# The opening rounds of a hybrid DeltaNet and sparse-attention decoder step: another order for blocks, splits, modulation tiles, block weights and constants

## The chip, the cores and the metric

The kernel runs on one core of a Trainium2 chip. Its engines work in parallel, each through its own queue of instructions in order: TensorE (PE; its weight loads are shown as PEld), VectorE (DVE), ScalarE (ACT), GpSimd (POOL) and SyncE (SP), which issues most of the transfers. The metric is the device time of one execution in microseconds; 2323.8 is the median of three runs of the kernel before.

## The reference, cut to what matters

One layer: a modulated, normalised input `h` goes through one wide projection `w_in`, feeds two branches (gated DeltaNet, and attention over keys that an indexer selects), and their merge goes through an output projection.

```
mod = einsum('bc,cd->bd', silu(c), w_ada) + b_ada        # 9 conditionings, 2048 x 6144
shift, scale, gate = split(mod, 3)
h = rms_norm(x, pre_norm_g) * (1 + scale) + shift        # 256 prompt + 64 sample tokens
(a_qkv, a_z, a_b, a_a, b_q, b_k, b_v, b_z, i_q, i_k, i_w, g_a, g_b) = split_columns(h @ w_in)
y_a = gdn_branch(a_qkv, a_z, a_b, a_a, ...)
y_b = attend(b_q, b_k, b_v, i_q, i_w, i_k) * silu(b_z)
merged = sigmoid(g_a) * (y_a @ w_pa) + sigmoid(g_b) * (y_b @ w_pb)
out = x + gate * rms_norm(merged @ w_out, post_norm_g)
```

All is float32. `h` is needed by every product with `w_in`, and it needs `shift` and `scale`, which are two thirds of the product with `w_ada`: 32 MB of weights for 9 rows.

## The kernel before

The 320 tokens (256 prompt, 64 sample) lie along the free axis. An operand of 128 features is kept as two parts, `xh` (rounded to a format that TensorE takes in one pass) and `xl` (the remainder); weights are split in the same way into `whi`/`wlo`, by ScalarE (a copy that rounds) and VectorE (the difference). A product of one 128 x 128 block is three matmuls: hi by xh, hi by xl, lo by xh.

`build` plans a stream of chunks of `w_in`, `w_pa`, `w_pb` and `w_out`. A chunk is 256 columns in two half tiles `raw` of 1 MB each; it gives four units of 24 matmuls (`stream`), each unit with its own `whi`/`wlo`. `split_ahead` keeps two units split ahead, `load_ahead` asks for `raw` tiles when one of three is free. Attention, recurrence and gates are generators beside the stream; `side_round` runs them in the middle and at the end of a unit, when a model of the engines' clocks (`Clock`) says that their inputs are ready. The order of instructions on every engine's queue is the order in which the program emits them.

`startup` comes ahead of the stream. It has eight rounds. Round q takes two column blocks of `w_ada` (256 columns of shift, 256 of scale), in four tiles of 1 MB (`rawx`, `raw`), through a ring of six buffers, three of its own and the three `raw` tiles. The product with the conditionings `cT` uses four 32-column groups of the array at once; "columns" below means these products, 64 instructions per round, 16 per tile. Their sums in `pm` are copied to `msb`, four matmuls with `sel` add the groups, VectorE makes `mod` and `gs`, and `operand` transposes two blocks of `x` and makes two 128-feature blocks of `xh` and `xl` (helper `hT`).

`first_blocks(q)` uses the two feature blocks of round q for the first 720 columns of `w_in` (step sizes, indexer weights and key, attention's k and v): a tile `awr` of 128 x 2 x 720, filled by four transfers per round, split into `awh` and `awl`, and 36 matmuls into six accumulators `ps`. In round q the order is: all columns of round q, the copy to `msb`, `first_blocks(q-1)` with its split at its head, selection, operands. Two PSUM banks (`ps_main`) serve columns, selection and transposes in turn.

The requests for tiles come from `load`, which is called after the columns and in `first_blocks`; it asks for block weights as early as two modulation tiles ahead of the count. After the rounds `attention` opens its buffers, loads the page table, makes row numbers (`idx`), a selection matrix `esel`, masks and constants on POOL and VectorE, and starts the side work; only then are the six accumulators copied out and the stream begins.

Nearly every instruction of the trace has line 56, that of a helper which records all operations, so groups are told apart by tile names.

Of the kernel before, what the change touches and what calls it, by code (L numbers as in the profile page):

```python
# [7 lines left out]
F32 = mybir.dt.float32  # L8
F32R = mybir.dt.float32r
BF = mybir.dt.bfloat16  # L10
I32 = mybir.dt.int32
AF = mybir.ActivationFunctionType
OP = mybir.AluOpType
AX = mybir.AxisListType
# [3 lines left out]
NP = 256  # L18
NB, TS = 8, 8
NS = NB * TS  # L20
NT = NP + NS
KB = D // 128
PAGES = 8
# [167 lines left out]
class Kernel:  # L191
# [254 lines left out]
    def startup(self):  # L446
        nc, i = self.nc, self.i
# [17 lines left out]
        def load():  # L465
            while True:
                if st["w"] < min(8, (st["a"] + 2) // 4) and awr.free:
                    load_w()
                if st["a"] == len(seq) or not ring.free:
                    break  # L470
                q, h = seq[st["a"]]
                t = ring.get()
                nc.sync.dma_start(t, wa[1024 * h:1024 * (h + 1), 256 * q:256 * (q + 1)].rearrange(
                    "(k p) c -> p k c", p=128))
                raws[q, h] = t
                st["a"] += 1

        def load_w():
            q = st["w"]
            t = awr.get()  # L480
            for d0, c0, n in ((0, C_BA, 64), (64, C_IW, 16), (80, C_IK, 128), (208, C_BK, 512)):
                nc.sync.dma_start(t[:, :, d0:d0 + n], w[256 * q:256 * (q + 1), c0:c0 + n].rearrange(
                    "(k p) c -> p k c", p=128))
            aws[q] = t
            st["w"] += 1
# [29 lines left out]
        self.sel = self.l0.tile([128, 9], F32, name="sel")  # L515
        nc.vector.tensor_reduce(self.sel, self4, axis=AX.X, op=OP.add)

        junk = self.xh.rearrange("p k t -> p (k t)")[:, 0:D]
# [17 lines left out]
        accs = [self.ps_side.get() for _ in range(6)]  # L536
        blocks = [(0, 80, self.aux_done), (80, 128, self.ik_done)]
        blocks += [(208 + 128 * n, 128, lambda p, n=n: self.bk_done(p, n)) for n in range(2)]
        blocks += [(464 + 128 * n, 128, lambda p, n=n: self.bv_done(p, n)) for n in range(2)]

        def first_blocks(q):
            r = aws.pop(q)
            hi, lo = awh[q % 2], awl[q % 2]
            self.act(hi, r)
            self.tt(lo, r, hi, OP.subtract)
            awr.put(r)
            load()
            for e in range(2):
                kb = 2 * q + e
                for (c0, n, _), acc in zip(blocks, accs):  # L550
                    a = acc[:n, :NT]
                    wh, wl = hi[:, e, c0:c0 + n], lo[:, e, c0:c0 + n]
                    nc.tensor.matmul(a, wh, self.xh[:, kb, :], start=(kb == 0), stop=False)
                    nc.tensor.matmul(a, wh, self.xl[:, kb, :], start=False, stop=False)
                    nc.tensor.matmul(a, wl, self.xh[:, kb, :], start=False, stop=(kb == KB - 1))

        for q in range(8):
            p = self.ps_main.get()
            for e, qq in enumerate((q, 8 + q)):
                for k in range(KB):  # L560
                    j = k % 4
                    self.mm(p[32 * j:32 * j + 32, 256 * e:256 * e + 256], self.cT[:, k, :],
                            raws[qq, k // 8][:, k % 8, :], start=(k < 4), stop=(k >= 12), skip=True)
                for h in range(2):
                    t = raws.pop((qq, h))
                    if q < 6 or t in own:
                        ring.put(t)
                    else:
                        self.raw.put(t)
            load()  # L570
            if q == 7:
                self.load_ahead()
            m = msb
            self.act(m, p)
            self.ps_main.put(p)
            if q == 0:
                p = self.ps_main.get()
                self.tr(p[:, 0:81], rows)
                nc.vector.tensor_copy(self.feat, p[:, 0:81])
                self.ps_main.put(p)  # L580
            if q > 0:
                first_blocks(q - 1)
            p = self.ps_main.get()
            for e in range(4):
                self.mm(p[:, 9 * e:9 * e + 9], m[:, 128 * e:128 * e + 128], self.sel)
            bc = lambda a, n: a.rearrange("p (e o) -> p e o", o=1).to_broadcast([128, n, 9])
            for e, qq in enumerate((q, 8 + q)):
# [5 lines left out]
                     OP.add, OP.mult)  # L593
            for k in (k0, k0 + 1):
                self.operand(k, x, gs, mod, hT[k % 2])
        first_blocks(7)
# [104 lines left out]
    def attn_small(self):  # L701
# [8 lines left out]
        self.att = set()  # L710

    def attention(self):
        nc, a, i = self.nc, self.ap, self.i
        self.qiS = a.tile([128, NB, 128], F32, name="qiS")
# [7 lines left out]
        self.wip = a.tile([128, 2, 16], F32, name="wip")  # L722
        self.esel = a.tile([64, NB, 16, TS], BF, name="esel")
        self.q_r = Ring([a.tile([128, NP], F32, name=f"q{j}") for j in range(6)])
# [4 lines left out]
        self.st = Ring([a.tile([128, 8], F32, name=f"st{j}") for j in range(6)])  # L729

        self.idx = a.tile([128, NB], I32, name="idx")
        pt = a.tile([128, NB], I32, name="pt")
        for s in range(PAGES):
            nc.gpsimd.dma_start(pt[16 * s:16 * s + 16, :],
                                i["page_table"][:, s:s + 1].rearrange("b o -> o b").to_broadcast([16, NB]))
        io = a.tile([128, NB], I32, name="io")
        nc.gpsimd.iota(io, pattern=[[0, NB]], base=0, channel_multiplier=1)
        pgi = a.tile([128, PAGES - 1], I32, name="pgi")
        nc.gpsimd.iota(pgi, pattern=[[-16, PAGES - 1]], base=-16, channel_multiplier=1)
        pgf = a.tile([128, PAGES - 1], F32, name="pgf")  # L740
        nc.vector.tensor_scalar(pgf, pgi, 0.0, None, op0=OP.is_ge)
        page = a.tile([128, 1], F32, name="page")
        nc.vector.tensor_reduce(page, pgf, axis=AX.X, op=OP.add)
        ptf = a.tile([128, NB], F32, name="ptf")
        nc.vector.tensor_scalar(ptf, pt, page, 16.0, op0=OP.subtract, op1=OP.mult)
        self.stt(self.idx, ptf, 1.0, io, OP.mult, OP.add)
        nc.vector.memset(self.esel, 1.0)
        nc.gpsimd.affine_select(self.esel, self.esel, pattern=[[-8, NB], [0, 16], [-1, TS]], compare_op=OP.is_equal,
                                fill=0.0, base=0, channel_multiplier=1)
        self.wi_consts()  # L750
        self.aux_masks()
        self.aux_setup()
# [25 lines left out]

    def wi_consts(self):
        nc, a = self.nc, self.ap  # L780

        self.hsp = a.tile([128, 16, 8], F32, name="hsp")
        e = self.hsp[64:80]
        nc.vector.memset(self.hsp[64:96], 1.0)
        nc.gpsimd.affine_select(e, e, pattern=[[8, 16], [0, 8]], compare_op=OP.is_equal, fill=0.0, base=0,
                                channel_multiplier=-8)
        dti = a.tile([128, 8, 16], I32, name="dti")
        nc.gpsimd.iota(dti, pattern=[[-1, 8], [-8, 16]], base=0, channel_multiplier=1)
        dt = self.s_r.get()
        dtf = dt[:, 0:128].rearrange("p (t h) -> p t h", t=8)  # L790
        nc.vector.tensor_scalar(dtf, dti, 0.0, None, op0=OP.is_equal)
        self.tmask = a.tile([128, 8], F32, name="tmask")
        nc.vector.tensor_reduce(self.tmask, dtf, axis=AX.X, op=OP.add)
        self.s_r.put(dt)

    def aux_masks(self):
        nc, f, a = self.nc, self.fix, self.ap
        g, v, m = nc.gpsimd, nc.vector, self.mask
# [30 lines left out]
    def aux_gen(self):  # L829
# [10 lines left out]
        p = self.psum()  # L840
        self.mm(p[:, 0:64], self.hsp[64:80].rearrange("p h t -> p (h t)"), ax[64:80, NP:NT])
        self.ts(self.wsel, p[:, 0:64].rearrange("p (b t) -> p b t", t=TS), 0.25, None, OP.mult)
        self.tt(self.wsel, self.wsel,
                self.tmask.rearrange("p (o t) -> p o t", o=1).to_broadcast([128, NB, TS]), OP.mult)
        self.ps_side.put(p)
        self.ts(self.wip, xt[:, 0:2, 64:80], 0.25, None, OP.mult)
        self.flags.add("wi")
# [4 lines left out]
        nc.sync.dma_start(al[:, 32:64], i["dt_bias"].to_broadcast([128, 32]))  # L852
        self.act(self.beta, xt[:, :, 0:32], AF.Tanh, scale=0.5)
        self.act(al[:, 0:32], al[:, 0:32], AF.Exp)
# [4 lines left out]
        g = a.tile([128, 3, 32], F32, name="g")  # L859
        self.tt(t1, xt[:, :, 32:64], rep(al[:, 32:64]), OP.add)  # L860
        self.stt(t2, t1, -1.0, t1, OP.mult, OP.min)
# [1273 lines left out]
```

## Time and profile before

| | |
|---|---|
| three runs | 2316.94, 2323.8, 2326.34 us |
| the profiled execution | 2320.8 us, of which the span of the trace is 2319.1 us |
| TensorE busy | 2216.6 us (96% of the span) |
| VectorE, ScalarE, POOL busy | 1368.6, 1013.4, 469.4 us |
| transfers | 432.96 MB, mean 187 GB/s |

Rows of the trace are read like this: windows give busy time of each engine in a stretch with the number of instructions in brackets; a chain row is a start, a duration, and the engine and tile whose work the end of the kernel waited for; a timeline row has a start, a duration, engine, operation, out<-in, and in square brackets the idle time ahead of it and what ended it.

### The profile page before, as it was taken

Reading aid. Unit: us, or ns where it says so; the run is one execution under the profiler, and the core shown is the slowest. Engines: PE = TensorE matmul, PEld = TensorE weight load, DVE = VectorE, ACT = ScalarE, POOL = GpSimd, SP = SyncE. Lnnn points to the kernel's source line nnn. Section 1 sums busy time; section 2 is a strip of 40 time slices with the busy share of each in tenths; the row PEclk is TensorE's granted clock in tenths of the full one; section 3 lists DMA queues with packets and bytes.
Section 4 is the critical chain, followed back from the end, with each engine's and each line's share of the span. In section 5 each row is a group of like instructions: output and inputs, shape, how many; then the busy total and the mean of one; then the engine's idle time right before and its main releaser. Section 6 shows DMA issues by size and latency. Waiting matters only on the chain.

```text
span 2319.1 us, 41332 instructions
## 1 busy us (share of the span) xinstructions
PE 2216.6 (96%) x16448; PEld 2081.1 (90%) x16448; DVE 1368.6 (59%) x2666; ACT 1013.4 (44%) x2191; POOL 469.4 (20%) x624
## 2 busy tenths in 40 slices
PE   5779999999999999999999999999999999999997
PEld 2658997999988999898989898989899999999997
DVE  2323345788844467685868586858665554545433
ACT  2123346443333354554556464546553543333342
POOL 0010000000000007072627162727171000000000
PEclk9878999999999999999999999999999999999999
DMA  9958743434455556475756565656574866644443
GB/s 324 323 162 257 236 162 104 165 110 134 149 202 197 195 177 210 131 237 146 225 169 205 165 208 169 205 168 206 165 231 142 273 210 198 196 153 156 159 142 103
DMA packets 475137, 432.96 MB, mean 187 GB/s; under 512 B 65912, under 2 KB 463880, under 8 KB 472576
## 3 DMA queue, kind: packets, MB, share of 16 engines
q1 hardware_dynamic: 470560, 406.61, 56.3%
q0 software_dynamic: 3840, 21.02, 2.5%
q8 instruction: 129, 2.11, 0.4%
q10 hardware_dynamic: 544, 2.70, 0.3%
q14 instruction: 64, 0.52, 0.1%
HBM read 382.10 MB, written 47.89 MB: 185 GB/s over the span
## 4 chain that ended last, share of the span: by engine, by line
PE 80%; DVE 10%; ACT 4%; POOL 2%; DMA 2%; issue 2%; DVEq 0%; SPq 0%; POOLq 0%; ACTq 0%
PE pm L56 65%; PE ps L56 15%; DVE S L56 2%; DVE wlo L56 2%; DVE ps L56 1%; POOL X L56 1%; ACT whi L56 1%; POOL tmpx L56 1%; DMA raw<-in_w_ada_dram 1%; DMA rawx<-in_w_ada_dram 1%; ACT ot L56 1%; DVE st L56 1%; DVE w L56 1%; DVE awl L56 1%; ACT ps L56 1%
## 5 line engine op out<-in xcount | busy, mean ns | idle before, releaser
L56 PE MATMUL pm<-xh,whi 128*128 128x320 f32 x3328 | 1065.6, 320 | 3.9 <-ACT whi L56 3.9
L56 PE MATMUL pm<-xh,wlo 128*128 128x320 f32 x3328 | 1033.4, 311 | 12.2 <-DVE wlo L56 12.1
L56 PE MATMUL pm<-xl,whi 128*128 128x320 f32 x3328 | 1031.2, 310 | 0.0
L56 DVE TENSOR_TENSOR wlo<-raw,whi 128x1024 fp32r<-128x1024 f32 x480 | 601.9, 1258 | 372.7 <-ACT whi L56 370.9
L56 PEld LDWEIGHTS pm<-xh,whi 128*128 128x128 f32 x3328 | 628.7, 189 | 35.4 <-issue 25.6
L56 PEld LDWEIGHTS pm<-xh,wlo 128*128 128x128 f32 x3328 | 627.9, 189 | 15.2 <-DVE wlo L56 15.0
L56 PEld LDWEIGHTS pm<-xl,whi 128*128 128x128 f32 x3328 | 628.8, 189 | 1.0
L56 ACT ACTIVATE whi<-raw 128x1024 fp32r<-128x1024 f32 x480 | 504.2, 1056 | 261.8 <-PE pm L56 227.5
L56 POOL TENSOR_TENSOR X<-X,tmpx 48x31 f32<-48x31 f32 (+15 forms) x248 | 182.8, 737 | 19.4
L56 POOL TENSOR_TENSOR tmpx<-blk,X 48x31 f32<-48x31 f32 (+15 forms) x248 | 170.7, 688 | 44.3 <-DMA blk<-d_b 25.8
L56 PE MATMUL pm<-y1h,wlo 128*128 128x320 f32 x512 | 157.9, 308 | 0.7 <-DVE wlo L56 0.7
L56 PE MATMUL pm<-y1l,whi 128*128 128x320 f32 x512 | 157.9, 308 | 0.1
L56 PE MATMUL pm<-y1h,whi 128*128 128x320 f32 x512 | 158.0, 309 | 0.0
L56 POOL TENSOR_TENSOR sc<-sc,mh 128x6 f32<-128x6 f32 (+1 forms) x24 | 42.4, 1766 | 438.7 <-DVE sc L56 425.0
L56 DVE SCALAR_TENSOR_TENSOR ps<-xp,cs,ps 128x344 f32<-128x344 f32 x192 | 111.5, 581 | 6.8
L56 POOL TENSOR_TENSOR rfin<-rfin,mh 128x3 f32<-128x3 f32 x1 | 0.8, 850 | 496.2 <-DVE rfin L56 496.2
L56 PEld LDWEIGHTS pm<-y1h,wlo 128*128 128x128 f32 x512 | 96.0, 187 | 1.0 <-DVE wlo L56 1.0
L56 PEld LDWEIGHTS pm<-y1l,whi 128*128 128x128 f32 x512 | 95.9, 187 | 0.3 <-DVE y1l L56 0.3
L56 PEld LDWEIGHTS pm<-y1h,whi 128*128 128x128 f32 x512 | 96.0, 187 | 0.3 <-ACT y1h L56 0.2
L56 ACT ACTIVATE vt<-ps,sc 128x128 f32<-128x128 f32 (+1 forms) x112 | 42.5, 410 | 81.7 <-DVE w L56 64.9
L56 DVE SCALAR_TENSOR_TENSOR S<-S,gtr,ps 128x128 f32<-128x128 f32 x256 | 67.5, 342 | 0.7 <-PE ps L56 0.4
L56 ACT ACTIVATE xp<-pm 128x256 f32<-128x256 f32 (+1 forms) x128 | 31.9, 302 | 71.7 <-PE pm L56 71.5
(310 smaller groups left out, 2332.7 us busy)
## 6 DMA issues: line engine op xcount, KB each, us to landing
raw<-in_w_in_dram SPq DMA_DIRECT2D x176, 1024.0 KB
raw<-in_w_pa_dram SPq DMA_DIRECT2D x32, 1024.0 KB
rawx<-in_w_ada_dram SPq DMA_DIRECT2D x17, 1024.0 KB
a<-in_w_ada_dram SPq DMA_DIRECT2D x16, 1024.0 KB
S<-in_state_gdn_dram SPq DMA_DIRECT2D x32, 512.0 KB
out_dram<-S SPq DMA_DIRECT2D x32, 512.0 KB
raw<-in_w_pb_dram SPq DMA_DIRECT2D x16, 1024.0 KB
raw<-in_w_out_dram SPq DMA_DIRECT2D x16, 1024.0 KB
```

The lines of the kernel that those rows point to most:

```text
L56: made = fn(*args, **kw)
```

## The change

Inside a round, the columns are taken tile by tile (`columns`), and each tile is followed by a call of `load`. Between the tiles stands other work: selection of the round before behind the first tile, its operands and `first_blocks` behind the second, and the split of this round's block weights (now `split`, apart from `first_blocks`) behind the third. The columns' PSUM bank is held over the whole round. The last round's rest follows the loop, with the first three `raw` tiles asked for and two units of the stream split ahead of the last blocks. The transposed bias and norm rows (`feat`) are made ahead of round 0. Block weights are asked for only once four modulation tiles are, and come in three transfers instead of four, since indexer key and weights are neighbours in `w_in`; the auxiliary rows change places for it (indexer weights at partitions 0 to 15 in place of 64 to 79). Constants and masks of `attention` are made ahead of the rounds (`attn_consts`), the page table is fetched in round 2 and the row numbers are computed in round 5.

```
         def load():
             while True:
-                if st["w"] < min(8, (st["a"] + 2) // 4) and awr.free:
+                if st["a"] >= 4 and st["w"] < min(8, (st["a"] + 2) // 4) and awr.free:
                     load_w()
...
-            for d0, c0, n in ((0, C_BA, 64), (64, C_IW, 16), (80, C_IK, 128), (208, C_BK, 512)):
+            for d0, c0, n in ((0, C_IK, 144), (144, C_BA, 64), (208, C_BK, 512)):
...
+        then = self.attn_consts(sp, th)
...
-        def first_blocks(q):
+        def split(q):
             r = aws.pop(q)
             hi, lo = awh[q % 2], awl[q % 2]
             self.act(hi, r)
             self.tt(lo, r, hi, OP.subtract)
             awr.put(r)
-            load()
+
+        def first_blocks(q):
+            hi, lo = awh[q % 2], awl[q % 2]
...
+        def columns(q, e, h, p):
+            t = raws.pop((q + 8 * e, h))
+            for k in range(8):
+                kb, j = 8 * h + k, k % 4
+                self.mm(p[32 * j:32 * j + 32, 256 * e:256 * e + 256], self.cT[:, kb, :], t[:, k, :], start=(kb < 4),
+                        stop=(kb >= 12), skip=True)
+            if q < 6 or t in own:
+                ring.put(t)
+            else:
+                self.raw.put(t)
             load()
...
+        p = self.ps_main.get()
+        self.tr(p[:, 0:81], rows)
+        nc.vector.tensor_copy(self.feat, p[:, 0:81])
+        self.ps_main.put(p)
+        for q in range(8):
+            p = self.ps_main.get()
+            columns(q, 0, 0, p)
+            if q > 0:
+                factors(q - 1)
+            columns(q, 0, 1, p)
+            if q > 0:
+                for k in (2 * q - 2, 2 * q - 1):
+                    self.operand(k, x, gs, mod, hT[k % 2])
+                first_blocks(q - 1)
+            columns(q, 1, 0, p)
+            split(q)
+            load()
+            columns(q, 1, 1, p)
+            self.act(msb, p)
+            self.ps_main.put(p)
+            if q in then:
+                then[q]()
+        self.load_ahead(now=True)
+        factors(7)
+        for k in (14, 15):
+            self.operand(k, x, gs, mod, hT[k % 2])
+        self.split_ahead(2)
         first_blocks(7)
...
+    def attn_consts(self, sp, free):
...
+        self.wi_consts(sp, free)
+        self.aux_masks()
+        return {2: fetch, 5: rows}
```

`factors(q)` is the selection with `mod` and `gs`, unchanged in itself. `attn_consts` holds the lines that stood in `attention` from `idx` to `aux_masks`.

## Rows read from the trace of the kernel before

**Rows 1.** Windows: stretch, its length, busy us per engine, granted clock, DMA share, GB/s.
```profile
0.00:20.00 20.00, 3.06 (x22) 1.16 (x26) 2.95 (x16) 7.82 (x9) 3.99 (x13) 1.00 0.94 283
20.00:85.00 65.00, 47.56 (x384) 32.17 (x377) 18.46 (x41) 9.17 (x14) 0.88 (x1) 0.97 1.10 345
85.00:150.00 65.00, 51.74 (x445) 40.96 (x444) 19.18 (x48) 11.31 (x16) 0.00 (x0) 0.83 0.86 268
150.00:168.00 18.00, 12.90 (x71) 11.83 (x70) 5.12 (x14) 4.04 (x8) 4.49 (x10) 0.77 0.01 0
168.00:178.00 10.00, 2.25 (x10) 1.73 (x9) 5.24 (x13) 3.65 (x5) 3.44 (x5) 0.69 0.66 210
...
200.00:250.00 50.00, 50.00 (x416) 43.23 (x409) 19.60 (x35) 21.47 (x45) 0.00 (x0) 1.00 0.92 292
```

**Rows 2.** Waits of TensorE from 200 us on: total us, times, longest.
```profile
PE ps L56 <- ACT w L56: 12.3, 7, 2.2
PE pm L56 <- DVE wlo L56: 6.5, 8, 2.1
```

**Rows 3.** Chain of waits, a round of the opening and blocks of a later one.
```profile
64.75 5.22 PE ps L56 x34
...
72.11 3.71 PE pm L56 x64
...
76.39 1.40 ACT awh L56
77.81 1.67 DVE awl L56
...
112.15 7.52 PE ps L56 x34
```

**Rows 4.** Chain of waits, last round, constants, first units of the stream.
```profile
153.81 0.81 PE pm L56 x8
...
171.33 2.03 POOL esel L56
...
175.37 1.24 DVE wlo L56
176.65 3.03 PE pm L56 x10
...
221.25 3.51 PE pm L56 x24
```

**Rows 5.** Timeline, last matmul of the stream's first half-unit.
```profile
183.73 0.47 PE L56 MATMUL pm<-xh,wlo 128*128 128x320 f32 x1
```

**Rows 6.** Timeline, the operands of the last round.
```profile
155.22 0.54 DVE L56 TENSOR_SCALAR hT<-pm,gs,mod 128x256 f32<-128x256 f32 x1
...
156.19 0.47 ACT L56 ACTIVATE xh<-hT 128x320 fp32r<-128x320 f32 x1 [11.63 <-DVE hT L56]
156.69 0.49 DVE L56 TENSOR_TENSOR xl<-hT,xh 128x320 fp32r<-128x320 f32 x1 [0.54 <-ACT xh L56]
...
158.06 0.47 ACT L56 ACTIVATE xh<-hT 128x320 fp32r<-128x320 f32 x1 [1.40 <-DVE hT L56]
```

**Rows 7.** Transfers from 0 to 200 us: GB/s in 40 slices; a small load, us to landing.
```profile
GB/s 169 396 304 261 350 349 338 348 349 348 348 331 347 349 328 353 348 284 297 348 335 211 353 334 149 362 204 182 262 161 0 0 0 18 351 52 335 253 256 212
...
rows<-in_gdn_norm_g_dram POOLq DMA_DIRECT2D x1, 0.5 KB, 6.4
```

**Rows 8.** Windows: the granted clock (last but two) in a gap and the blocks behind it.
```profile
79.00:80.00 1.00, 0.47 (x2) 0.47 (x3) 0.47 (x1) 0.00 (x0) 0.00 (x0) 0.87 1.09 346
80.00:81.00 1.00, 1.00 (x5) 1.00 (x5) 0.00 (x0) 0.00 (x0) 0.00 (x0) 0.50 1.10 349
...
83.00:84.00 1.00, 1.00 (x8) 1.00 (x8) 0.00 (x0) 0.00 (x0) 0.00 (x0) 0.93 1.10 347
```

**Rows 9.** Timeline of the first 20 us: columns of one tile, the last sum of squares.
```profile
8.62 1.94 PE L56 MATMUL pm<-rawx,cT 128*32 128x256 f32 x16 [0.47 <-DVE cT L56]
...
18.09 1.91 ACT L56 ACTIVATE xh<-x 64x2048 fp32r<-64x2048 f32 x1 [1.36 <-DMA x<-in_x_sample_dram]
```

More of the change, by code (lines that the diff above doesn't have):

```diff
@@ L536, in startup @@
         accs = [self.ps_side.get() for _ in range(6)]
-        blocks = [(0, 80, self.aux_done), (80, 128, self.ik_done)]
+        blocks = [(128, 80, self.aux_done), (0, 128, self.ik_done)]
         blocks += [(208 + 128 * n, 128, lambda p, n=n: self.bk_done(p, n)) for n in range(2)]
         blocks += [(464 + 128 * n, 128, lambda p, n=n: self.bv_done(p, n)) for n in range(2)]
-        def first_blocks(q):
+        def split(q):
             r = aws.pop(q)
@@ L555, in first_blocks, with factors @@
                     nc.tensor.matmul(a, wl, self.xh[:, kb, :], start=False, stop=(kb == KB - 1))
[L557 to L569, printed above, removed]
-            load()
[L571 to L582, printed above, removed]
+        def columns(q, e, h, p):
[8 more added lines that the diff above has]
+                self.raw.put(t)
+            load()
+        def factors(q):
             p = self.ps_main.get()
             for e in range(4):
-                self.mm(p[:, 9 * e:9 * e + 9], m[:, 128 * e:128 * e + 128], self.sel)
+                self.mm(p[:, 9 * e:9 * e + 9], msb[:, 128 * e:128 * e + 128], self.sel)
             bc = lambda a, n: a.rearrange("p (e o) -> p e o", o=1).to_broadcast([128, n, 9])
@@ L593, in startup @@
                      OP.add, OP.mult)
-            for k in (k0, k0 + 1):
-                self.operand(k, x, gs, mod, hT[k % 2])
+        p = self.ps_main.get()
[25 more added lines that the diff above has]
+        self.split_ahead(2)
         first_blocks(7)
@@ L710, in attn_small, with fetch, rows @@
         self.att = set()
+    def attn_consts(self, sp, free):
+        nc, a, i = self.nc, self.l0, self.i
+        self.esel = a.tile([64, NB, 16, TS], BF, name="esel")
+        self.idx = a.tile([128, NB], I32, name="idx")
+        pt = a.tile([128, NB], I32, name="pt")
+        io = a.tile([128, NB], I32, name="io")
+        nc.gpsimd.iota(io, pattern=[[0, NB]], base=0, channel_multiplier=1)
+        pgi = a.tile([128, PAGES - 1], I32, name="pgi")
+        nc.gpsimd.iota(pgi, pattern=[[-16, PAGES - 1]], base=-16, channel_multiplier=1)
+        pgf = a.tile([128, PAGES - 1], F32, name="pgf")
+        nc.vector.tensor_scalar(pgf, pgi, 0.0, None, op0=OP.is_ge)
+        page = a.tile([128, 1], F32, name="page")
+        nc.vector.tensor_reduce(page, pgf, axis=AX.X, op=OP.add)
+        ptf = a.tile([128, NB], F32, name="ptf")
+        def fetch():
+            for s in range(PAGES):
+                nc.gpsimd.dma_start(pt[16 * s:16 * s + 16, :],
+                                    i["page_table"][:, s:s + 1].rearrange("b o -> o b").to_broadcast([16, NB]))
+        def rows():
+            nc.vector.tensor_scalar(ptf, pt, page, 16.0, op0=OP.subtract, op1=OP.mult)
+            self.stt(self.idx, ptf, 1.0, io, OP.mult, OP.add)
+        nc.vector.memset(self.esel, 1.0)
+        nc.gpsimd.affine_select(self.esel, self.esel, pattern=[[-8, NB], [0, 16], [-1, TS]], compare_op=OP.is_equal,
+                                fill=0.0, base=0, channel_multiplier=1)
+        self.wi_consts(sp, free)
+        self.aux_masks()
+        return {2: fetch, 5: rows}
     def attention(self):
-        nc, a, i = self.nc, self.ap, self.i
+        a = self.ap
         self.qiS = a.tile([128, NB, 128], F32, name="qiS")
@@ L722, in attention @@
         self.wip = a.tile([128, 2, 16], F32, name="wip")
-        self.esel = a.tile([64, NB, 16, TS], BF, name="esel")
         self.q_r = Ring([a.tile([128, NP], F32, name=f"q{j}") for j in range(6)])
@@ L729, in attention @@
         self.st = Ring([a.tile([128, 8], F32, name=f"st{j}") for j in range(6)])
[L731 to L751, printed above, removed]
         self.aux_setup()
@@ L777, in attn_end, with wi_consts @@
         self.shut("attn0")
-    def wi_consts(self):
-        nc, a = self.nc, self.ap
+    def wi_consts(self, sp, free):
+        nc, a = self.nc, self.l0
         self.hsp = a.tile([128, 16, 8], F32, name="hsp")
-        e = self.hsp[64:80]
-        nc.vector.memset(self.hsp[64:96], 1.0)
+        e = self.hsp[0:16]
+        nc.vector.memset(self.hsp[0:32], 1.0)
         nc.gpsimd.affine_select(e, e, pattern=[[8, 16], [0, 8]], compare_op=OP.is_equal, fill=0.0, base=0,
                                 channel_multiplier=-8)
-        dti = a.tile([128, 8, 16], I32, name="dti")
+        dti = sp.tile([128, 8, 16], I32, name="dti")
         nc.gpsimd.iota(dti, pattern=[[-1, 8], [-8, 16]], base=0, channel_multiplier=1)
-        dt = self.s_r.get()
-        dtf = dt[:, 0:128].rearrange("p (t h) -> p t h", t=8)
+        dtf = free[:, 0, :].rearrange("p (t h) -> p t h", t=8)
         nc.vector.tensor_scalar(dtf, dti, 0.0, None, op0=OP.is_equal)
@@ L793, in wi_consts @@
         nc.vector.tensor_reduce(self.tmask, dtf, axis=AX.X, op=OP.add)
-        self.s_r.put(dt)
     def aux_masks(self):
-        nc, f, a = self.nc, self.fix, self.ap
+        nc, f, a = self.nc, self.fix, self.l0
         g, v, m = nc.gpsimd, nc.vector, self.mask
@@ L840, in aux_gen @@
         p = self.psum()
-        self.mm(p[:, 0:64], self.hsp[64:80].rearrange("p h t -> p (h t)"), ax[64:80, NP:NT])
+        self.mm(p[:, 0:64], self.hsp[0:16].rearrange("p h t -> p (h t)"), ax[0:16, NP:NT])
         self.ts(self.wsel, p[:, 0:64].rearrange("p (b t) -> p b t", t=TS), 0.25, None, OP.mult)
@@ L845, in aux_gen @@
         self.ps_side.put(p)
-        self.ts(self.wip, xt[:, 0:2, 64:80], 0.25, None, OP.mult)
+        self.ts(self.wip, xt[:, 0:2, 0:16], 0.25, None, OP.mult)
         self.flags.add("wi")
@@ L852, in aux_gen @@
         nc.sync.dma_start(al[:, 32:64], i["dt_bias"].to_broadcast([128, 32]))
-        self.act(self.beta, xt[:, :, 0:32], AF.Tanh, scale=0.5)
+        self.act(self.beta, xt[:, :, 16:48], AF.Tanh, scale=0.5)
         self.act(al[:, 0:32], al[:, 0:32], AF.Exp)
@@ L859, in aux_gen @@
         g = a.tile([128, 3, 32], F32, name="g")
-        self.tt(t1, xt[:, :, 32:64], rep(al[:, 32:64]), OP.add)
+        self.tt(t1, xt[:, :, 48:80], rep(al[:, 32:64]), OP.add)
         self.stt(t2, t1, -1.0, t1, OP.mult, OP.min)
```

## The prediction, made before the changed kernel ran

> **What bounds the kernel now.** I read the busy times by stretch first, then TensorE's waits, the chain of waits through the opening, and last transfers and clock. TensorE is the engine with hardly a gap: from 200 to 250 us it is busy 50.00 of 50 us [rows 1], and behind 200 us its longest wait in total, on ScalarE's `w`, is 12.3 us [rows 2]. What is taken out ahead of that stretch should therefore come off the end. The opening is the exception. From 20 to 85 us the DMA engines move 345 GB/s at full share; from 85 to 150 us only 268, with TensorE busy 51.74 of 65; from 150 to 168 us nothing moves, and from 168 to 178 us TensorE is busy 2.25 of 10 us [rows 1]. The chain shows why. A round is columns 3.71 (64 instructions), the block weights' rounding on ScalarE 1.40, their remainder on VectorE 1.67 and 34 block matmuls, 5.22 in one round and 7.52 in a later one [rows 3], and behind them selection, 0.81 [rows 4]: a serial ring. After the last round VectorE and POOL make page-row and mask constants (`esel` 2.03); the first `wlo` starts only at 175.37, and the stream of weights in earnest at 176.65 [rows 4]. Its first half-unit of 24 matmuls ends at 183.73 + 0.47 = 184.2 us [rows 5].
>
> **The change, part by part.** The sum goes by the profiled execution, 2320.8 us (span 2319.1 and 1.7 around it), 3 us under the median of 2323.8.
>
> *Rounds and splits.* `split(q)` now runs while the same round's tiles are consumed, so the 1.40 + 1.67 us leave TensorE's path. What is late next is one of two things.
> (a) Transfers: four 1024 KB tiles and one block-weight tile of 256 x 720 x 4 B are 4.93 MB, at 345 GB/s 14.3 us.
> (b) TensorE's own order: four tiles of columns at 0.93, selection 0.81, operands, 36 block matmuls. The open columns hold one of the two PSUM banks all round, so both operands go through the other, and no block may start before its `xh` and `xl`. Before `hT` at 155.22 stand 0.8 us of transposes; the first `xl` is done at 156.69 + 0.49, 2.7 us after the first transpose; the second operand follows 1.9 us behind (`xh` 156.19, then 158.06) [rows 6], under the first 18 block matmuls. So 3.7 + 0.8 + 2.7 + 5.3 = 12.5 us at the high clock.
> 14.3 against 12.5: transfers set the pace. A tile is asked for as soon as its buffer's column products are done; six buffers are 18 us of transfers and the longest pause between two releases is 8 us, so the DMA should not run dry. SP's queue has the block weights four tiles or more ahead of their split, and its wait for their buffer (the split two rounds back) is past by then.
>
> *When the rounds end.* By 20 us 283 GB/s x 20 = 5.66 MB have moved [rows 1]. Up to the second tile of the last round there are 30 tiles (31.46 MB), seven block-weight tiles (5.16), x and c (2.69): 39.31 MB, so 20 + 33.65/0.345 = 117.5 us. For landing I allow 1.5 us, between 0 and the 6.4 us of a small load on POOL's queue [rows 7], nearer to 0 because a queue kept full hides it. From 119.0: columns 0.9, operands and blocks of round 6 2.7 + 5.3, the last two tiles 1.9 (landed by 127): 129.8.
>
> *Tail.* msb 0.65; from selection to `xl` 3.4 (153.81 to 157.18) [rows 4, 6]; then 36 blocks. In that gap TensorE has 2 us of work, much as in the gaps of before, where the granted clock fell from 1.00 to 0.50 (2.4 to 1.2 GHz) between 79 and 81 us and was 0.93 at 83 [rows 8]: so I take 7.5 for the blocks, not 5.3. End 141.4; with the clock kept 139.1. The three freed weight tiles are asked for behind the last modulation tile on SP's queue and land 3 us apart, at about 130, 133, 136. `split_ahead(2)` stands on ScalarE and VectorE behind the operands, runs under the blocks, and delays nothing but the accumulators' copies, which the stream does not wait for. Unit 0 follows without a pause: 3.51 us for 24 matmuls [rows 4] and 0.6 of side work, ending at 145.5. That is 38.7 us ahead of 184.2.
>
> *Constants moved to the start.* Some 11 VectorE and 7 POOL instructions now stand ahead of the sums of squares and hold VectorE until about 15 us, `esel` alone 2.03. ScalarE's squares wait on a memset behind them, but the last of x is there only at 18.09 [rows 9]. Cost 0 to 2 us on a chain that round 1 needs near 30: 0, and 2 if that cover were gone. The eight page-table loads go to POOL's queue in round 2, where nothing else waits; the index arithmetic in round 5 finds them landed. The `feat` transpose now stands first on TensorE and waits for small loads (6.4 us to land), so the first columns start near 12 and not at 8.62 us [rows 9]; the six buffers cover it.
>
> *Three transfers for four.* 20 to 85 us as a whole runs at 345 GB/s, the best bins of 5 us at 349 [rows 1, 7]: block weights cost at most 1% of 121 us, 1.4 us, and one transfer fewer gains between 0 and that. I take 0, since the pace of 345 holds them already. The Trainium skill's page "DMA: Bandwidth & Descriptors" (Anatomy of one DMA) puts a fixed 2.0 us on each DMA beside its bytes; eight fewer would be 16 us by that, an estimate. The trace, with four such transfers inside each round at 345 GB/s, does not bear that out.
>
> *Aux rows and `hsp` at partitions 0 to 15:* the same instructions, nothing either way. *Later side work:* the planner enters the stream with other clocks and may order side work differently, which the trace can't show. Bounds: 8 us lost or gained, a fifth of the waits and start of the stream; the two largest waits are 12.3 and 6.5 [rows 2]. I take 0.
>
> Sum: 2320.8 - 38.7 = 2282.1 on the profiled run, 2285.1 on the median; I say 2283.
>
> **The rivals.**
> 1. *The clock falls in every round, which then goes at TensorE's pace.* Blocks at 7.5 instead of 5.3 and half the tiles at 1.94 [rows 9] instead of 0.93 make 12.5 + 2.2 + 2.0 = 16.7 us, 2.4 above the transfers; over six rounds 14 us: 2297. For it: the clock did fall in the later rounds of before. Against: those gaps held 0.5 us of work in 3.7; the new ones are shorter or filled.
> 2. *The stream gives back.* Before, three weight tiles and 18 us of silent DMA preceded the stream; now it starts with one or two tiles landed and the gate's loads on top, in a phase that ran the DMA at 0.92 share [rows 1]. Price: two tiles at 3 us and a worse side order, 8 to 14 us in all: 2293. Against: TensorE had no gap at that share.
> 3. *Slower: low clock throughout.* Columns now come in pieces of one tile, each followed by a wait on a transfer or an operand. Were the clock at 1.2 GHz from the first round to the tail, a round is 4 x 1.94 + 1.6 + 3.3 + 2 x 5.3 = 23.3 us. Round 0 ends at about 25, seven rounds at 188, the tail takes 15 and unit 0 8: 211 against 184.2, so 2347. It decides from rounds of 19.5 us on. Against it: every run of block matmuls of before brought the clock back. The Trainium skill's page "TensorE: Matmul & The Clock Gate" (HAM oscillation) tells of short bursts between transfer waits that each start at the halved clock; by that rule this rival would be the outcome. The trace agrees only with the fall, not with a clock that stays down.
> 4. *More than forecast:* the clock holds through the tail and the side order falls out better: 2271 to 2276.
>
> **How the numbers follow.** Forecast 0.60 (own range 2275 to 2291), rival 1 0.13, rival 2 0.14, rival 3 0.05, rival 4 0.08. Within 0.5% (11.6 us, about what a measurement of this kernel can tell from no change) lie 0.02 of rival 1, with colder rounds, and 0.01 of rival 3. So faster 0.93, same 0.03, slower 0.04. The range 2271 to 2301 takes in rivals 1, 2 and 4 and leaves out rival 3 and the tails.
>
> **What would show it.** Right: DMA near 345 GB/s from 20 to 125 us without the dip from 85 on; rounds 14.3 us apart; `awl` no longer among TensorE's long waits; last columns at about 130, blocks done between 139 and 142, no POOL select ahead of the first `wlo`; waits behind the first unit unchanged. Wrong: rounds above 16 us with a granted clock of 0.50 in the columns; TensorE waiting for `raw` or `a` in the first 50 us of the stream; waits in the rest well above those of before.

## The result and the profile after

The changed kernel takes 2293.39 us (median of 4, 2290.62 to 2295.61) where the kernel before takes 2321.32: a ratio of 0.9881 (95% interval 0.9864 to 0.9898). Timed again beside later runs it was 2295.21 against 2320.85, 0.9895 (0.9879 to 0.9910). So 26 to 28 us went; 38.7 were forecast. The profiled execution took 2290.6 us, with a span of 2288.9: 30.2 less than before. A second profiled execution of the same kernel took 2296.3.

The windows of the changed kernel, to be held against [rows 1] (columns as there):

```profile
0.00:20.00 20.00, 4.03 (x31) 1.72 (x35) 5.48 (x26) 7.11 (x8) 7.38 (x20) 1.00 0.92 279
20.00:85.00 65.00, 51.44 (x433) 35.51 (x424) 21.49 (x49) 11.66 (x17) 7.30 (x9) 0.97 1.03 325
85.00:125.00 40.00, 36.87 (x336) 28.46 (x336) 13.68 (x35) 8.03 (x11) 0.00 (x0) 0.91 1.10 349
125.00:150.00 25.00, 21.42 (x143) 18.00 (x139) 11.21 (x24) 9.24 (x15) 0.00 (x0) 0.86 0.68 217
...
160.00:178.00 18.00, 15.21 (x111) 12.73 (x110) 4.15 (x9) 8.06 (x22) 0.00 (x0) 0.91 0.67 213
...
200.00:250.00 50.00, 50.00 (x408) 43.53 (x408) 17.88 (x30) 15.96 (x29) 2.04 (x2) 1.00 0.81 261
```

The transfers no longer sag from 85 us on (349 GB/s up to 125), but they are at 325 from 20 to 85, where before had 345. The slices of 5 us show where:

```profile
GB/s 133 390 319 272 340 339 138 314 349 343 349 349 316 353 349 334 349 350 347 351 348 344 350 348 350 349 349 273 2 110 357 350 348 295 79 133 365 349 352 351
```

The seventh slice, 30 to 35 us, moves 138 GB/s; [rows 7] has no such hole there. The chain of waits, for [rows 3, 4]:

```profile
70.06 11.62 DMA raw<-in_w_ada_dram
...
85.43 6.90 PE ps L56 x35
...
92.33 5.30 PE pm L56 x75
...
99.67 6.89 PE ps L56 x35
...
112.43 11.60 DMA raw<-in_w_ada_dram
...
124.07 1.66 PE pm L56 x19
...
127.77 5.37 PE ps L56 x35
133.14 1.91 PE pm L56 x32
...
138.98 5.79 PE ps L56 x21
...
162.81 6.70 DMA al<-in_dt_bias_dram
...
175.12 1.24 DVE wlo L56
```

Splits have left the chain. The two tiles of the chain landed at 81.68 and 124.03, three rounds apart at 14.1 us each, and were used at once, so the transfers set the pace. But TensorE had no slack left: from 85.43 to 99.67 blocks, columns and operands take 14.2 us with no transfer among them, and from 57 to 118 us TensorE waits for no tile at all (its waits there are 3.8 us on `hT` and 0.8 on `xl`). The stream's first matmul is at 146.78 and its first half-unit ends at 152.4 [rows 5: 184.2]:

```profile
146.78 0.31 PE L56 MATMUL pm<-xh,whi 128*128 128x320 f32 x1
...
152.11 0.31 PE L56 MATMUL pm<-xh,wlo 128*128 128x320 f32 x1
```

Behind it TensorE's waits are those of [rows 2], and one on the gate's tiles:

```profile
PE ps L56 <- ACT w L56: 12.2, 7, 2.2
PE pm L56 <- DVE wlo L56: 6.3, 7, 2.1
...
PE ps L56 <- DMA a<-in_w_ada_dram: 1.5, 2, 1.0
```

### The profile page after: what moved, and what is told of

Same layout as the page of the kernel before. It is cut to its first block, busy times and chain, and to the rows that moved or that the text cites. A ratio compares the mean times of both kernels' runs of the same rounds, so it can differ in the third digit from the quotient of the medians.

```text
span 2288.9 us, 41315 instructions
## 1 busy us (share of the span) xinstructions
PE 2207.7 (96%) x16448; PEld 2072.5 (91%) x16448; DVE 1368.2 (60%) x2666; ACT 1012.9 (44%) x2191; POOL 470.6 (21%) x624
## 4 chain that ended last, share of the span: by engine, by line
PE 77%; DVE 10%; ACT 4%; DMA 4%; POOL 2%; issue 1%; SPq 1%; DVEq 0%; POOLq 0%; ACTq 0%
PE pm L56 63%; PE ps L56 14%; DVE S L56 2%; DVE wlo L56 2%; DMA raw<-in_w_ada_dram 2%; SPq L56 1%; ACT whi L56 1%; DVE ps L56 1%; POOL X L56 1%; POOL tmpx L56 1%; ACT ot L56 1%; DVE w L56 1%; ACT ps L56 1%; DVE st L56 1%; DMA raw<-in_w_in_dram 0%
## 5 line engine op out<-in xcount | busy, mean ns | idle before, releaser
L56 POOL TENSOR_TENSOR X<-X,tmpx 48x31 f32<-48x31 f32 (+15 forms) x248 | 182.9, 738 | 19.4
```

Source lines behind the costliest of these rows:

```text
L56: made = fn(*args, **kw)
```

## Experiments

Times are medians beside the kernel before on the same chip (2318.9 to 2320.9). The changed kernel's 2293.4 and 2295.2 are the yardstick. Where two times lie too close, one can compare when the same matmul of the stream starts in two traces, here the 2400th that reads `whi` or `wlo`: at 648.64 us before, at 621.15 and 622.22 in the two profiled executions of the changed kernel.

**Which part makes the pace: the early split.** In `e3_split_late` the split goes back to the head of the blocks.

```
                     self.operand(k, x, gs, mod, hT[k % 2])
+                split(q - 1)
+                load()
                 first_blocks(q - 1)
             columns(q, 1, 0, p)
-            split(q)
-            load()
             columns(q, 1, 1, p)
...
+        split(7)
         self.split_ahead(2)
```

> The changed kernel, but block weights are split at the head of the blocks that use them, one round later, behind the operands, as before; tile order, constants and transfers as changed. Theory (transfers set the pace at 14.3 us a round, TensorE's own order takes 12.5): with 1.4 + 1.7 us back on TensorE's path a round takes some 15 to 15.6 us once behind the transfers, so the blocks end 5 to 9 us later and the kernel takes 2298 to 2302. Rival (the split was the whole gain in the rounds): rounds near 16.5 us, 2306 or more. Rival (transfers hide it): no more than 2 us.

2331.5 us, ratio 1.0048 (1.0030 to 1.0066): 36 to 38 us lost, the whole gain and more. The 5 to 9 us missed; the first rival's 2306 or more holds, its rounds of 16.5 us don't. Its chain, one round:

```profile
105.13 7.68 PE ps L56 x34
112.81 5.30 PE pm L56 x75
...
118.14 0.69 DVE hT L56 x2
...
119.11 0.48 ACT xh L56
...
119.61 0.49 DVE xl L56
120.10 0.60 DVE hT L56 x2
...
121.36 1.40 ACT awh L56
...
122.78 1.67 DVE awl L56
...
124.49 6.65 PE ps L56 x34
```

From 105.13 to 124.49 it is 19.4 us, and all of it serial; the mean of five rounds, from 67.12 to 162.12, is 19.0. My sum had 12.5 + 3.1. It lacked that the split, behind both operands in ScalarE's and VectorE's queues, brings the second operand's 1.9 us onto the path too, and that TensorE, idle for 5 us, loses its clock (granted 0.50, which is 1.2 GHz, from 121 to 127 us), with blocks at 6.60 to 7.88 in all these rounds, not 5.3. That is more than a round of before (14.8 to 17.1), where the operands ran under the next columns: moved blocks without a moved split are a loss. This run also shows what the rival of rounds from 19.5 us on would have looked like: slower than before.

**The places between tiles.** In `e6_tiles_first` the four tiles of a round come first, the early split stays.

```
-            columns(q, 0, 0, p)
+            for e in range(2):
+                for h in range(2):
+                    columns(q, e, h, p)
             if q > 0:
                 factors(q - 1)
-            columns(q, 0, 1, p)
-            if q > 0:
...
                 first_blocks(q - 1)
-            columns(q, 1, 0, p)
             split(q)
             load()
-            columns(q, 1, 1, p)
```

> The changed kernel, but in every round all four tiles of columns come first and then selection, operands and blocks of the round before, and the split of this round's block weights: the blocks are not placed between tiles, the rest is as changed. Theory (the early split makes the pace, the places between tiles only let the last round's wait hide the blocks of round 6): rounds still 14 to 14.5 us, the last blocks end some 6 to 8 us later, 2298 to 2301 against 2293. Rival (the places between tiles are what keeps the transfers running): rounds above 15.5 us, the dip in the transfers back, 2305 or more. Rival (nothing hangs on the places): within 2 us of 2293.

2306.3 us, 0.9946 (0.9929 to 0.9964): 11 to 13 us lost, over the theory's number. Rounds take 14.5 us, the mean of five from 67.69 to 140.21, and the transfers run at 348 GB/s from 85 to 125 us. So the signs of the first rival, rounds above 15.5 us and the dip, are absent, though its time (2305 or more) was met:

```profile
67.69 7.03 PE ps L56 x36
82.12 6.57 PE ps L56 x36
96.10 7.95 PE ps L56 x36
111.75 6.89 PE ps L56 x35
...
140.21 8.08 PE ps L56 x36
```

The blocks of round 6 begin only at 140.21, past all tiles, and those of round 7 follow them; the stream begins at 158.5, 11.7 us later than in the changed kernel. What the placing hides is, in the main, one round's blocks under the wait for the last two tiles. The rounds themselves go at TensorE's pace here: from 57 to 118 us it waits for VectorE alone, and for no tile.

**The constants alone**, in the kernel before (`e5_consts_only`): `attn_consts` ahead of the sums of squares, the page table fetched behind the rounds.

```
+        self.attn_consts(sp, th)
         junk = self.xh.rearrange("p k t -> p (k t)")[:, 0:D]
...
-        self.wi_consts()
-        self.aux_masks()
+        self.fetch_pages()
```

> The kernel before with one part of the change alone: constants and masks are made ahead of the rounds; the page table is still fetched and the row numbers computed after them (the latter some units into the stream). Theory: the stall ahead of the first wlo goes (from the selects and the page table, 168.8 to 175.4 us), so the stream starts 5 to 6 us earlier and the kernel takes some 2315 on the scale of 2320.5; nearly all the rest of the changed kernel's 28 us is the rounds'. Rival: what starts earlier waits again for the gate's and the decay parameters' loads, within 1 us of 2320.5. Rival: the constants are the larger part, 2305 or less.

2314.1 against 2318.9, 0.9973 (0.9957 to 0.9988): 5 us, as the theory had it. The chain, for [rows 4]:

```profile
156.60 0.81 PE pm L56 x8
...
172.59 1.24 DVE wlo L56
```

From the last selection to the first `wlo` it is 16.0 us, where it was 21.6 before: the 5.6 us of the stall. The first `wlo` itself is only 2.8 us earlier, because the rounds of this execution end 2.8 us later (blocks from 64 us on at 6.75, not 5.22; that the constants do this is not shown). At the stream's 2400th matmul (644.82) 3.8 us are gained.

**Three transfers or four** (`e2_four_loads`).

```
-            for d0, c0, n in ((0, C_IK, 144), (144, C_BA, 64), (208, C_BK, 512)):
+            for d0, c0, n in ((0, C_IK, 128), (128, C_IW, 16), (144, C_BA, 64), (208, C_BK, 512)):
```

> The changed kernel, with the block weights of a round again in four transfers (the 144 columns of indexer key and weights as 128 and 16, to the same places). Theory (the prediction's): 0 to 1.4 us slower over eight rounds, rounds at the same 14 us. Rival (a fixed price of about 2 us per transfer that stands in the transfers' path): up to 16 us slower, the eight rounds each 2 us longer. Rival B of the other run (the three transfers make the dip at 31 to 36 us): the dip goes and the kernel is up to 5 us faster.

2291.2, 0.9881 (0.9859 to 0.9904): no difference, and the hole from 31 to 36 us is there as well (104 GB/s). Neither a price of 2 us each, 16 us in all, nor a benefit can be seen; the 2400th matmul starts at 620.91.

**The hole at 31 us: page-table loads.** In the changed kernel they are written down for round 2, but nothing on POOL's queue holds them until then, and they go out in round 0:

```profile
21.94 6.45 POOL L56 DMA_DIRECT2D pt<-in_page_table_dram x8
...
29.43 10.91 SPq L56 DMA_DIRECT2D rawx<-in_w_ada_dram x3
...
38.28 1.94 PE L56 MATMUL pm<-raw,cT 128*32 128x256 f32 x16 [3.81 <-DMA raw<-in_w_ada_dram]
```

`e1_page_late` gives them a tile whose space the opening still uses; `fetch` then stands in `attention`, `rows` some units into the stream.

```
         def fetch():
+            pt = self.pt = self.ap.tile([128, NB], I32, name="pt")
...
-        return {2: fetch, 5: rows}
+        self.page = fetch, rows
+        return {}
```

> The changed kernel, but the eight page-table loads again write a tile of the attention buffers, so that they cannot start before the last round, and the row numbers are computed some units into the stream. Theory A (the page-table loads, issued at 21.9 us beside full tile transfers, leave a few DMA engines behind, so that the tile waited for until 38.2 us comes late): the DMA dip from 31 to 36 us goes, that tile lands by about 33, the second tile of the last round is used at 119 to 120 instead of 124.1, and the kernel is 4 to 5 us faster than the changed kernel (2288 to 2289 on its median scale of 2293). Rival B (the dip belongs to the opening itself: x, block weights in three transfers and tiles in one full queue): the dip stays, the tile at 38, the time within 1 us of 2293.

`e7_pages_twice` keeps them and issues the eight loads a second time.

```
+            for s in range(PAGES):
+                nc.gpsimd.dma_start(pt2[16 * s:16 * s + 16, :],
+                                    i["page_table"][:, s:s + 1].rearrange("b o -> o b").to_broadcast([16, NB]))
```

> The changed kernel with the eight page-table loads issued twice in the opening (the first time into a tile that nothing reads). Theory A (these small loads leave a few DMA engines behind, and tiles are whole only when the slowest engine is through): the stretch of low transfer rate from 31 us on doubles, from 5 to about 10 us, and the columns of the second tile of round 1 start at 42 to 45 instead of 38.3 us. Rival (something else at that place): the dip stays 5 us long.

The windows of `e1_page_late` and of `e7_pages_twice`:

```profile
31.00:36.00 5.00, 5.00 (x35) 2.79 (x27) 0.44 (x3) 0.00 (x0) 0.00 (x0) 1.00 1.09 351
```

```profile
31.00:36.00 5.00, 3.10 (x22) 2.01 (x12) 0.44 (x3) 0.00 (x0) 1.60 (x4) 1.00 0.37 116
36.00:41.00 5.00, 2.34 (x18) 0.88 (x18) 0.00 (x0) 0.00 (x0) 0.53 (x1) 1.00 0.38 120
41.00:50.00 9.00, 8.23 (x36) 7.21 (x36) 2.95 (x9) 2.35 (x3) 0.00 (x0) 1.00 0.68 223
```

Without them the hole is gone (351 GB/s) and the stream begins at 142.7, 4.1 us earlier; doubled, the hole goes on past 41 us and the stream begins at 156.4, 9.6 us later (one execution, 2303.0). The other traces agree: from 31 to 36 us six executions with the loads move 93 to 166 GB/s, four without them 351 to 360. So the loads make the hole: that is shown. The tile of 38.3 us did not come later with twice the loads (38.66), against the expectation; it was the tiles after it. Through the doubled hole the DMA share is 0.37, a third of the 1.10 at full rate, and in the changed kernel SP stands for 10.91 us in issuing three tiles, 6.27 in `e1_page_late`. I read it as a few engines behind with the small loads and the queue waiting for them; that is not shown, and which engines, no row says.

But the end hardly moved: `e1_page_late` took 2292.1, 0.9869 (0.9853 to 0.9886), not to be told from the changed kernel's 0.9881, and its 2400th matmul starts at 619.56, 1.6 us earlier. Most of the 4.1 us had been lost again by 174, by the chain and by TensorE's waits in the stream:

```profile
161.99 6.51 DMA al<-in_dt_bias_dram
...
174.11 1.24 DVE wlo L56
```

```profile
PE ps L56 <- DMA a<-in_w_ada_dram: 3.2, 2, 3.0
```

The wait of 3.0 us is TensorE's, for the gate's first tile at 151.4 us, with a granted clock of 0.66 from 150 to 160; in the changed kernel the longest such wait is 1.0.

**The second wait in the row: two small parameter loads.** The generator of the decay factors loads `a_log` and `dt_bias` on SP's queue at 158.1, behind gate and weight tiles, and ScalarE's exponential waits for them in its queue with `whi` behind it. In the changed kernel:

```profile
169.20 0.23 ACT L56 ACTIVATE al<-al 128x32 f32<-128x32 f32 x1 [10.05 <-DMA al<-in_a_log_dram]
```

Before, that wait was 4.0 us and TensorE did not notice. `e4_al_early` loads them at the start, and those on SP's queue go (a small mask moves to another tile to make room).

```
+        self.al = self.l0.tile([128, 64], F32, name="al")
+        nc.scalar.dma_start(self.al[:, 0:32], i["a_log"].to_broadcast([128, 32]))
+        nc.scalar.dma_start(self.al[:, 32:64], i["dt_bias"].to_broadcast([128, 32]))
```

> The changed kernel, with the two small loads of the decay parameters asked for at the start, on ScalarE's queue behind x, instead of in the stream on SP's queue. Theory (these loads, behind weight and gate tiles in the full SP queue from 158 to 169 us, hold ScalarE for 10.1 us, and with it whi, until TensorE waits and falls to 1.2 GHz at 172 to 180): ScalarE's wait goes, TensorE has no gap from 164 to 178 and no low clock there, 3 to 6 us faster than the changed kernel: 2287 to 2290. Rival (TensorE has two units split ahead and rides it out): within 1 us of 2293.

2290.5, 0.9869 (0.9853 to 0.9886). Against the changed kernel's 0.9881 the times alone can't tell, but the fifth `wlo` comes at 164.49 instead of 175.12, TensorE has a granted clock of 1.00 from 160 to 178 us, and the 2400th matmul starts at 616.97, 4.2 us earlier:

```profile
164.49 1.23 DVE L56 TENSOR_TENSOR wlo<-raw,whi 128x1024 fp32r<-128x1024 f32 x1 [2.08 <-ACT whi L56]
```

Both together are `b_both`:

> The changed kernel with both repairs: page-table loads after the rounds, decay parameters loaded at the start. Alone the first moved the first unit 4.1 us earlier and nothing came out at the end, the second took ScalarE's wait out and gave 2 to 3 us. Theory C (two waits in series: the parameter loads had swallowed the earlier start): both together give 6 to 8 us, 2285 to 2287. Rival D (behind the first unit the transfers are the bound, since gate tiles and stream weights together ask for all that the DMA gives until about 195 us): 2 to 4 us as with the second alone, 2289 to 2291, with TensorE waiting for gate or weight tiles from 150 to 200.

2287.2, 0.9856 (0.9837 to 0.9875): theory C's number, but the trace does not bear theory C out. The 2400th matmul starts at 618.68, 2.5 us ahead of the changed kernel's and 1.7 behind that of `e4_al_early` alone. What swallows the earlier start is rival D's sign, for one tile only: the first gate product stands in TensorE's queue from 148.8 on, its tile can be loaded only when the opening's buffers are free, and the clock falls behind it (mean 0.66 from 150 to 160):

```profile
152.39 1.93 PE L56 MATMUL ps<-a,cT 128*32 128x256 f32 x16 [3.62 <-DMA a<-in_w_ada_dram]
```

`c_both_gates` spreads the gate's products (`yield self.later(4.0)` behind each tile):

> As the run with both repairs, and the gate's products with the modulation weights are spread out, each tile's turn coming 4 us or more later by the planner's clock, so that gate tiles take less of the transfers in the first 50 us of the stream. Rival D: TensorE's waits for gate tiles vanish and the kernel gains 2 to 4 us on the run with both repairs, 2284 to 2287. Theory C (the transfers are not the bound): no change against that run, within 1 us. Third: the gate's tiles share buffers with the sample branch, whose start is held up, and the kernel loses several us.

2296.2, 0.9898 (0.9881 to 0.9915; a fifth execution, of 10893.7 us beside four near 2296, is left out): the third case by its time. The first wait stays (3.7 us), and later side work shifts: TensorE waits 11.8 us on `wlo` instead of 7.1, and 2.0 on cache tiles. That the shared buffers do this is not shown. `d_gate_wait` only holds the first product back:

```
             yield self.ready(pend[0])
+            while self.iq_n < 2:
+                yield
```

> The run with both repairs, and the gate's first product waits until two heads of the indexer are done, so that TensorE, which takes its queue in order, no longer stands before a gate tile that can only be loaded once the opening's buffers are free (3.6 us of wait at 149 to 152 us, and a clock of 0.66 behind it). Theory: that wait and the low clock go, 4 to 6 us less than both repairs alone, 2281 to 2284 where the kernel before takes 2319. Rival: the weight tiles asked for at the same time are late as well, or the gate's later tiles put other side work back, 2286 to 2290.

2283.0, 0.9834 (0.9815 to 0.9852), beside 2295.2, 0.9895 (0.9879 to 0.9910), for the changed kernel on the same chip, of which this was expected:

> The changed kernel itself, beside the repaired one on the same chip: 0.988 of the kernel before, as before, 2290 to 2295 where the kernel before takes 2319.

TensorE has no gap from 150 to 200 us, and the clock stays:

```profile
150.00:160.00 10.00, 10.00 (x72) 9.82 (x71) 3.52 (x7) 7.58 (x18) 0.00 (x0) 1.00 0.84 257
160.00:178.00 18.00, 18.00 (x149) 15.57 (x148) 7.13 (x11) 6.42 (x12) 0.00 (x0) 1.00 0.91 291
```

This version beats both kernels: 38 us under the kernel before. Against `b_both` the intervals of the times overlap, but the 2400th matmul starts at 613.41, 5.3 us earlier, as the theory had it.

## Why the prediction came out as it did

The mechanism was right in the main: the splits left TensorE's path, the transfers set the pace, and nothing of POOL stands ahead of the first `wlo`. The size was too large: 38.7 us forecast, 30.2 on the profiled executions, 26 to 28 on the medians. The median of 2293.4 lies past the forecast's own range (2275 to 2291) and on rival 2's 2293. The stated range of 2271 to 2301 holds it because it takes in that rival, and to meet that rival's number was luck: half of what was lost (5.4 of 11.2 us) was lost ahead of the stream, where that rival loses nothing. Point by point, on the profiled executions:

| step | forecast | measured | lost |
|---|---|---|---|
| a round | 14.3 | 14.1 | |
| second tile of the last round used | 119.0 | 124.07 | 5.1 |
| last columns end | 129.8 | 135.05 | 0.1 |
| last blocks end | 141.4 | 146.8 | 0.2 |
| first half-unit ends | 145.5 | 152.4 | 1.5 |
| gain there | 38.7 | 31.8 | |
| gain at the stream's 240th matmul (235.51 to 208.07) | 38.7 | 27.4 | 4.3 |
| gain at the 2400th (648.64 to 621.15) | 38.7 | 27.5 | |
| gain at the end of the span | 38.7 | 30.2 | |

- **The largest term that was mis-sized is the pace of 345 GB/s from 20 us on** (325 were measured up to 85 us), and under it the page-table loads, which I cost at nothing because nothing else waits on POOL's queue. I had looked at who waits behind them, not at the DMA engines that they share, nor at when they are issued: place in the program was taken for time. Without them the second tile of the last round was used at 119.86, and the stream began 4.1 us earlier.
- *TensorE's own 12.5 us* held only where the clock did. `b_both`, whose rounds wait for no tile from 57 to 118 us, shows both cases in the rows below this list. From 69.23 to 81.94 it is 12.7 us, from there to 96.18 it is 14.2. So rival 1 came half true: the clock did fall in rounds, in the blocks (6.90 at 85 us in the changed kernel, 5.37 at 127) and not in the columns. It cost next to nothing in the changed kernel because the transfers need 14.1 us a round; the slack of 1.8 us that I counted on was not there.
- *Three transfers for four*, taken at 0, was right by `e2_four_loads`. The fixed 2.0 us that I took from the Trainium skill's page "DMA: Bandwidth & Descriptors" (Anatomy of one DMA) is given there for transfers that GpSimd issues, and these are SP's, so that run says nothing against the page.
- *Tail*: 7.5 for the last blocks was the right choice between 5.3 and 7.5; between 138 and 144 us the clock was at 0.50.
- *Unit 0 "without a pause"* was wrong by 1.5 us: in TensorE's queue the first side work stands ahead of the next matmuls, and it waited 0.96 us for a copy that stood behind `wlo` on VectorE, itself behind the accumulators' copies that I said nothing waits for.
- *Rival 2, the stream gives back*, came true in part: 4.3 us between the first half-unit and the 240th matmul, with unit 0's 1.5 us 5.8, not 8 to 14; my sum had later side work at 0. From 160 to 178 us TensorE is idle for 2.8 us and its granted clock is 0.91. The place was not the one I named (too few weight tiles) but two waits on transfers that had been covered by 18 us of silent DMA: `al` on ScalarE and the gate's first tiles on TensorE (1.5 us on `a`, a sign I had listed as one of being wrong). With the three repairs the kernel takes 2283.0, 12 us less than the changed kernel on the same chip and the number forecast. That is near, not proof of every term: at the 2400th matmul it is 35.2 us ahead of the kernel before, not 38.7.
- *Rival 3* did not occur, but e3 shows that its threshold was near: rounds of 19.0 us in the mean were slower than before.

```profile
69.23 5.36 PE ps L56 x35
...
81.94 6.89 PE ps L56 x35
...
96.18 6.89 PE ps L56 x35
```

The 30.2 us of the profiled executions are in part their draw. Up to the 2400th matmul the gain is 27.5, as the medians have it; the rest comes later, where the two kernels do the same work. The second profiled execution of the changed kernel is 1.1 us behind the first at that matmul and 5.7 at the end. Not settled: what makes executions of one kernel differ so, and which DMA engines the page-table loads hold up.

## What to carry to other kernels

When a phase becomes bound by transfers, price every transfer in it, small ones first, and ask what holds each back: with nothing to wait for, the page-table loads were issued at 21.9 us, in round 0, though the program names them in round 2. When a silent stretch of the DMA is removed, list the loads that used to land in it and what stands behind each in its engine's queue. Moving work between waits pays only if what it needs (here the split) moves ahead of it too.

## What the hardware showed that I had not expected

Eight loads of 0.5 KB cut the transfer rate for 5 us and more: from 31 to 36 us 93 to 166 GB/s with them, 351 to 360 without, and 116 to 120 for 10 us with sixteen. Of two broadcast loads of 16 KB asked for among full tiles, one took 4.6 us to issue (`a_log`) and the other 6.7 from its issue to its landing (`dt_bias`).
